# Fill order in the mixer: attention's q and k right after the k products, logits of both head parities in turn

## The chip, the cores and the metric

The kernel runs on one core of a Trainium2 chip, in one launch. The metric is the device time of that launch in microseconds. Three runs of the kernel before took 934.95, 940.38 and 941.58 us; the median is 940.38 us.

## What is computed

The reference is two transformer-like blocks on 256 tokens of width 1024, all in fp32. Only the mixer of the first block is touched by the change. Its input is normalised and multiplied by `w_in` (1024 x 3600), and the product is cut into pieces: attention's q, k, v (512 columns each), the 1536 columns that a causal convolution of width 4 and SiLU turn into q, k, v of a gated delta net, 512 columns of a gate z, and two small ones.

- Attention has 8 heads of 64. With 256 tokens there is one block of keys, so it is plain causal softmax attention with a bias by distance: `softmax(q k^T / 8 + bias) v`.
- The delta net has 8 heads of 64 and chunks of 64 tokens. Per chunk and head it forms `K K^T` under a decay, inverts a unit lower triangular 64 x 64 matrix, forms `Q K^T` under the decay, and then runs a scan over the four chunks, in which each chunk's state follows from the one before.
- Both outputs go, side by side, through `w_out`, a norm and a residual. The MLP of the first block and the whole second block follow and are the same in both kernels.

## The kernel before

**Products in three parts.** Each fp32 product with a large weight is made of three fp32r products: weight and activation are each split into a high part (a copy rounded to fp32r) and a low part (the rest). A weight slice of 128 x 1024 numbers comes by one DMA on SP's queue (`raw`, 3 buffers), ScalarE makes the high part `wh` (L146), VectorE the low part `wl` (L149); there are 6 buffers of each. `gemm_ch_steps` (L279) computes 128 output columns for all 256 tokens with one such slice: 24 matmuls (8 rows of `w_in` blocks times 3), half a PSUM bank. Two slices fill a bank, and then an evacuation runs. This document calls the work on one slice a piece. `gemm_tok_steps` works the other way around, with 12 matmuls of 512 columns to a slice.

**Two streams.** The delta net's own code stands in order in the body: decay factors, transposes and norms of k, the products `K K^T` and their mask (tile `m`), the inverse, transposes and norms of q, `Q K^T` (tile `at`), and the scan. Beside it runs a generator, `fill` (L653), which yields the wide products and attention, each with a weight in us. `go(x)` (L689) takes from the generator until weights of `x` are used up, or until a mark such as "k" or "q" has come by. So `fill` gives the order of the wide work, and the list `FILL` says how much of it is put between the steps of the delta net. In the code's order the first seven pieces (convolved k, then the first three of convolved q) stand ahead of `K K^T`; one more, the last of convolved q, stands behind it, then the first piece of convolved v, and then q is transposed (`tok_major`).

**The chain around q.** `tok_major(0, t)` transposes q to token rows (L786). `inv_norm` (L789) squares on ScalarE, sums on VectorE (`ssq`, then `ms`, L383), and takes the power -1/2 on GpSimd (tile `rnq`, through `rstd`, L381). VectorE then scales q (`fq`, `qn`, `qd`), TensorE turns the results (L802), and `pair_products` (L805) forms `Q K^T`.

**The chain of the inverse.** The masked products are stored (`md`), and read back as 16 x 16 blocks (`mb`, L899). GpSimd eliminates in 15 steps of two instructions (`tmpb`, `tb`), copies the result turned (`ub`), and SP stores `td` and `ud` (L906, L907). GpSimd then multiplies `m` with two level masks, four products (tile `b`). Two rounds on TensorE (`units`) finish the inverse. In the code, `rnq` stands ahead of the elimination, and the four mask products stand between it and `qn`.

**Attention.** `att_in(i)` makes q (i = 0, 1) or k (i = 2, 3) of four heads; ScalarE copies the bank to a tile `aqk`. `logits(a, e)` (L598) takes the two heads of parity `e` among the four of group `a`: parity 0 lies on partitions 0 to 63, parity 1 on 64 to 127. It makes four matmuls of contraction 64 into two banks of the pool "at" (2 banks), adds the bias on VectorE, and normalises. Its bias tile comes by a DMA on SP (L594). `probs_T` transposes the probabilities, `att_out` multiplies with v.

**What sets the order.** The code's order is a priority, not the order of issue. A planner sorts each engine's list in advance by its own durations: an instruction that the planner thinks ready is put ahead of an earlier one that it thinks is not. On the chip each engine then keeps its list: an instruction that has to wait holds all that stands behind it on the same engine or queue. Buffers of one tag (`t`, `g`, PSUM pools `mm` of 3 banks, `sd` of 3, `at` of 2) are shared by many tiles.

Of the kernel before, what the change touches and what calls it, by code (L numbers as in the profile page):

```python
# [18 lines left out]
S = 256  # L19
# [80 lines left out]
def body(ctx: ExitStack, tc: tile.TileContext, I: dict, cst: bass.AP, out: bass.AP, dbg=None):  # L100
    nc = tc.nc
    P = 128

    def dump(name, ap):
        if dbg is not None:
            dbg(name, ap)
# [14 lines left out]
    def T2(name, dt=F32, shape=None, tag="t"):  # L121
        return xpool.tile(shape or [P, 512], dt, tag=tag, name=nm(name), bufs=SLOTS[tag])
# [4 lines left out]
    def T1(name, tag="h"):  # L127
        return xpool.tile([P, 256], F32, tag=tag, name=nm(name), bufs=SLOTS[tag])

    def sm(name, n):  # L130
        return small.tile([P, n], F32, tag=f"{name}{n}", name=nm(name))

    def bank(tag):
        return psum.tile([P, 512], F32, tag=tag, name=nm(tag), bufs=BANKS[tag])

    def mmps():
        return bank("mm")

    def sdps():
        return bank("sd")  # L140

    def atps():
        return bank("at")

    def act(o, i, f, **kw):
        nc.scalar.activation(o, i, f, **kw)  # L146
# [4 lines left out]
    def stt(o, a, s, b, op0, op1):  # L151
        nc.vector.scalar_tensor_tensor(o, a, s, b, op0=op0, op1=op1)  # L152
# [18 lines left out]
    @contextmanager  # L171
    def after(what):

        if what in last:
            with tc.issue_after(last[what].ins):
                yield
        else:
            yield
# [28 lines left out]
    def C(name):  # L207
        o, w = COFF[name]
        return CT[o // 512][:, o % 512:o % 512 + w]
# [19 lines left out]
    def mm(o, a, b, start=True, stop=True):  # L229
        nc.tensor.matmul(o, a, b, start=start, stop=stop)  # L230
# [48 lines left out]
    def gemm_ch_steps(w, c0, X, evac):  # L279

        ps = mmps()
        for f in range(2):
            late_l = len(started) < LATE_L
            H, L = load_w(w, 0, 8, c0 + f * P, P)
            o = ps[:, f * 256:(f + 1) * 256]
            for k in range(8):
                XH, XL = X.at(k)
                mm(o, H[:, k, :], XH, k == 0, False)
                mm(o, H[:, k, :], XL, False, False)
                if not late_l:  # L290
                    mm(o, L[:, k, :], XH, False, k == 7)
            if late_l:
                for k in range(8):
                    mm(o, L[:, k, :], X.at(k)[0], False, k == 7)
            if f == 1:
                evac(ps)
            piece()
            yield 2.6
# [233 lines left out]
    QT, KT = [None] * 2, [None] * 2  # L532
# [3 lines left out]
    def qkv(i):  # L536

        def conv_evac(ps):
            acc = T2("acc", tag="j")
            y = T2("y", tag="n")  # L540
            xp = [ps[:, j * S:(j + 1) * S] for j in range(2)]
            a = [acc[:, j * S:(j + 1) * S] for j in range(2)]
            for j in range(2):
                act(a[j], xp[j], AF.Copy, scale=tap1(3, 2 * i + j))
            for tap, sh in ((2, 1), (1, 2), (0, 3)):
                for j in range(2):
                    stt(a[j][:, sh:], xp[j][:, :S - sh], tap1(tap, 2 * i + j), a[j][:, sh:], MUL, ADD)
            last["y"] = nc.scalar.activation(y, acc, AF.Silu)
            Y[i] = y.rearrange("p (j n) -> p j n", j=2)
            dump(f"y{i}", y)  # L550

        yield from gemm_ch_steps(w_in, 1536 + 256 * i, X, conv_evac)

    def att_in(i):
        def qk_evac(ps):
            s_ = T2("aqk")
            act(s_, ps, AF.Copy)
            (QT if i < 2 else KT)[i % 2] = s_.rearrange("p (a n) -> p a n", a=2)

        yield from gemm_ch_steps(w_in, 256 * i, X, qk_evac)  # L560

    def z_in():
        def z_evac(t, ps):
            Z[t] = T2("z")
            act(Z[t], ps, AF.Silu)

        yield from gemm_tok_steps(w_in, 3072, X, z_evac)

    def v_in():
        def v_evac(t, ps):  # L570
            V[t] = T2("av")
            act(V[t], ps, AF.Copy)

        yield from gemm_tok_steps(w_in, 1024, X, v_evac)
# [4 lines left out]
    def bias_in():  # L579
        relT = const.tile([32, 8], F32, name="relT")  # L580
        with after("pow"):
            nc.gpsimd.dma_start(relT, I["rel_bias"].rearrange("h b -> b h"))
        vps = sdps()
        mm(vps[:8, :256], relT, C("hot")[:32, :])
        vec = T2("vec", tag="j")
        nc.gpsimd.memset(vec, NEG)
        nc.vector.tensor_copy(vec[:8, 127:383], vps[:8, :256])
        nc.sync.dma_start(vd, vec[:8, :])

    def bias_tile(a, e):  # L590

        v = vd[:, :]
        b = T2("bias")
        nc.sync.dma_start(b, bass.AP(tensor=v.tensor, offset=v.offset + (4 * a + e) * 512,  # L594
                                       ap=[[1, P], [1024, 2], [1, 256]]))
        BIAS[a, e] = b.rearrange("p (a k) -> p a k", a=2)[:, :, ::-1]

    def logits(a, e):  # L598

        er = slice(e * 64, (e + 1) * 64)  # L600
        pl0, pl1 = atps(), atps()
        for j in range(2):
            q_, k_ = QT[a][er, j, :], KT[a][er, j, :]
            mm(pl0[:, j * P:(j + 1) * P], q_[:, 0:P], k_[:, 0:P])
            mm(pl1[:, j * S:(j + 1) * S], q_[:, P:S], k_)
        bs = BIAS[a, e]
        lg0, lg1 = T1("lg0", "k"), T2("lg1")
        l0 = lg0.rearrange("p (j k) -> p j k", j=2)
        l1 = lg1.rearrange("p (j k) -> p j k", j=2)
        stt(l0, pl0[:, 0:S].rearrange("p (j k) -> p j k", j=2), 0.125, bs[:, :, P:S], MUL, ADD)  # L610
        stt(l1, pl1.rearrange("p (j k) -> p j k", j=2), 0.125, bs, MUL, ADD)
        nm_, sm_, rs_ = sm("nmx", 4), sm("sme", 4), sm("rse", 4)
        nc.vector.tensor_reduce(nm_[:, 0:2], l0, axis=AX.X, op=MAX, negate=True)
        nc.vector.tensor_reduce(nm_[:, 2:4], l1, axis=AX.X, op=MAX, negate=True)
        for j in range(2):
            act(l0[:, j, :], l0[:, j, :], AF.Exp, bias=nm_[:, j:j + 1], accum_out=sm_[:, j:j + 1])
            act(l1[:, j, :], l1[:, j, :], AF.Exp, bias=nm_[:, 2 + j:3 + j], accum_out=sm_[:, 2 + j:3 + j])
        nc.vector.reciprocal(rs_, sm_)
        for j in range(2):
            nc.vector.tensor_scalar(l0[:, j, :], l0[:, j, :], rs_[:, j:j + 1], None, op0=MUL)  # L620
            nc.vector.tensor_scalar(l1[:, j, :], l1[:, j, :], rs_[:, 2 + j:3 + j], None, op0=MUL)
        LG[a, e] = l0, l1
        yield 1.3

    def probs_T(a, e):
        l0, l1 = LG[a, e]
        pt0, pt1 = T2("pt0"), T1("pt1", "k")
        pp, pp1 = atps(), atps()
        for j in range(2):
            nc.tensor.transpose(pp[:, j * S:j * S + P], l0[:, j, :], ident)  # L630
            nc.tensor.transpose(pp[:, j * S + P:(j + 1) * S], l1[:, j, 0:P], ident)
            nc.tensor.transpose(pp1[:, j * P:(j + 1) * P], l1[:, j, P:S], ident)
        act(pt0, pp, AF.Copy)
        act(pt1, pp1[:, 0:S], AF.Copy)
        PT[a, e] = pt0.rearrange("p (j n) -> p j n", j=2), pt1.rearrange("p (j n) -> p j n", j=2)
        yield 0.7
# [16 lines left out]
    def fill():  # L653
        yield from qkv(2)
        yield from qkv(3)
        yield "k"
        yield from qkv(0)
        bias_in()
        yield from qkv(1)
        yield "q"  # L660
        yield from qkv(4)
        yield from qkv(5)
        yield "v"
        bias_tile(0, 0)
        yield from att_in(0)
        yield from att_in(2)
        yield from logits(0, 0)
        bias_tile(0, 1)
        yield from att_in(1)
        yield from logits(0, 1)  # L670
        bias_tile(1, 0)
        yield from z_in()
        yield "z"
        yield from probs_T(0, 0)
        yield from att_in(3)
        yield from logits(1, 0)
        bias_tile(1, 1)
        yield from probs_T(0, 1)
        yield from v_in()
        yield from logits(1, 1)  # L680
        yield from att_out(0)
        yield from probs_T(1, 0)
        yield from w_out_steps(2)
        yield from probs_T(1, 1)
        yield from att_out(1)
# [300 lines left out]
    for t in range(2):  # L986
# [5 lines left out]
        for c in range(2):  # L992
            cr = slice(c * 64, (c + 1) * 64)
            pw = sdps()
            for h in range(8):
                hc = slice(h * 64, (h + 1) * 64)
                e, a = h % 2, h // 2
# [30 lines left out]
    for t in range(2):  # L1028
        po = sdps()
        vn = USB[t]  # L1030
        for c in range(2):
# [11 lines left out]
            if n < 3:  # L1043
# [4 lines left out]
                for e in range(2):  # L1048
                    er = slice(e * 64, (e + 1) * 64)
# [182 lines left out]
    for i in range(4):  # L1232
# [9 lines left out]
        for j in range(2):  # L1242
            f = 2 * i + j
            a = acc[:, j * S:(j + 1) * S]
# [141 lines left out]
```

## Time and profile before

| what | value |
|---|---|
| runs | 934.95, 940.38, 941.58 us; median 940.38 |
| the profiled execution | 941.93 us, of which the span of instructions is 940.0 |
| TensorE busy in the span | 913.8 us (97%) |
| VectorE, ScalarE, GpSimd busy | 559.6, 453.2 and 94.4 us |
| mean granted TensorE clock | 0.993 of full |
| the mixer in the trace | from about 10 us to about 198 us |

Busy shares are means over very different stretches. The mixer is a fifth of the span; the rest is long products in which TensorE never stops. In the rows below a time is microseconds from the start of the span, and "[1.81 <-DVE qn L149]" at the end of a row means that the engine stood idle for 1.81 us before it, until an instruction of VectorE that writes `qn` had ended. Matmuls overlap, so the distance from one start to the next, and not the duration, says what one costs.

### The profile page before, as it was taken

To read this page: it belongs to the slowest core of one execution; us is meant where nothing else is said; L and a number is where in the kernel's file an instruction comes from. 1 tells how busy PE (TensorE), PEld (TensorE's weight loads), DVE (VectorE), ACT (ScalarE), POOL (GpSimd) and SP (SyncE) were. 2 spreads that over 40 slices of the span, in tenths; PEclk is the share of its full clock that TensorE was granted. 3 is DMA by queue.
4 is the path that set the end of the run, shared out by engine and by line. 5 is a ranking of instruction groups with operands and counts; after the bars stand their busy time and mean duration, and the time that the engine had idled before them with its cause. 6 is when DMAs were issued, how large, how long until landed. Compare 5 with 4: busy or idle time off the path is not lost.

```text
span 940.0 us, 15151 instructions
## 1 busy us (share of the span) xinstructions
PE 913.8 (97%) x6096; PEld 812.4 (86%) x6096; DVE 559.6 (60%) x770; ACT 453.2 (48%) x639; POOL 94.4 (10%) x127
## 2 busy tenths in 40 slices
PE   7797999999999999999999999999999999999997
PEld 7697887778999888799988899988888789999886
DVE  3776535486766544768666675645457656555443
ACT  4744464256655443654545554345344545444432
POOL 4187001130000000203200000000000000000000
PEclk9999899999999999999999999999999999999999
DMA  8685542156765666577645466566474567665551
GB/s 216 183 198 148 146 157 90 45 162 174 215 189 190 215 192 197 155 217 210 181 115 176 133 176 184 163 209 191 157 235 142 172 194 201 186 187 185 182 177 45
DMA packets 176870, 161.98 MB, mean 172 GB/s; under 512 B 18916, under 2 KB 144152, under 8 KB 176800
## 3 DMA queue, kind: packets, MB, share of 16 engines
q1 hardware_dynamic: 174912, 155.96, 56.6%
q0 software_dynamic: 1728, 4.78, 1.6%
q8 instruction: 48, 0.79, 0.4%
q10 hardware_dynamic: 160, 0.27, 0.1%
q14 instruction: 22, 0.18, 0.0%
HBM read 158.07 MB, written 2.92 MB: 171 GB/s over the span
## 4 chain that ended last, share of the span: by engine, by line
PE 86%; DMA 4%; DVE 4%; ACT 2%; issue 2%; POOL 1%; SPq 0%; POOLq 0%; ACTq 0%; DVEq 0%
PE mm L230 71%; PE at L230 8%; PE sd L230 7%; DMA raw<-in_w_in_dram 3%; DVE wl L149 1%; DVE acc L152 1%; ACT wh L146 1%; PE sd L802 1%; DMA hs<-in_dec_b_dram 1%; DMA raw<-in_w_up_dram 1%; ACT junk L405 0%; PE sd L1195 0%; POOL r L410 0%; POOL rnk L149 0%; POOL rnq L149 0%
## 5 line engine op out<-in xcount | busy, mean ns | idle before, releaser
L149 DVE TENSOR_TENSOR wl<-raw,wh 128x1024 fp32r<-128x1024 f32 x285 | 348.4, 1227 | 263.5 <-ACT wh L146 262.2
L146 ACT ACTIVATE wh<-raw 128x1024 fp32r<-128x1024 f32 x287 | 302.2, 1056 | 352.3 <-PE mm L230 125.6
L230 PE MATMUL mm<-xTh,wh 128*128 128x256 f32 x960 | 273.1, 286 | 0.2
L230 PE MATMUL mm<-xTl,wh 128*128 128x256 f32 x960 | 272.4, 285 | 0.3 <-DVE xTl L475 0.2
L230 PE MATMUL mm<-xTh,wl 128*128 128x256 f32 x960 | 268.8, 285 | 0.0
L230 PEld LDWEIGHTS mm<-xTl,wh 128*128 128x128 f32 x960 | 185.3, 193 | 1.6 <-DVE xTl L475 0.7
L230 PEld LDWEIGHTS mm<-xTh,wh 128*128 128x128 f32 x960 | 185.2, 193 | 0.8 <-ACT xTh L474 0.6
L230 PEld LDWEIGHTS mm<-xTh,wl 128*128 128x128 f32 x960 | 183.4, 193 | 0.7 <-issue 0.5
L230 PE MATMUL mm<-wh,xTh 128*128 128x512 f32 x264 | 104.0, 394 | 1.2 <-ACT xTh L394 1.2
L230 PE MATMUL mm<-wh,xTl 128*128 128x512 f32 x264 | 103.2, 391 | 1.5 <-DVE xTl L397 1.5
L230 PE MATMUL mm<-wl,xTh 128*128 128x512 f32 x264 | 103.3, 391 | 0.0
L230 PE MATMUL mm<-wh,hidh 128*128 128x512 f32 x162 | 63.3, 391 | 0.1
L230 PE MATMUL mm<-wl,hidh 128*128 128x512 f32 x162 | 63.3, 391 | 0.0
L230 PE MATMUL mm<-wh,hidl 128*128 128x512 f32 x162 | 63.0, 389 | 0.0
L230 PEld LDWEIGHTS mm<-wh,xTl 128*128 128x128 f32 x264 | 49.6, 188 | 12.9 <-DVE xTl L397 2.8
L230 PEld LDWEIGHTS mm<-wh,xTh 128*128 128x128 f32 x264 | 49.6, 188 | 12.3 <-ACT xTh L394 1.9
L230 PEld LDWEIGHTS mm<-wl,xTh 128*128 128x128 f32 x264 | 49.6, 188 | 10.4 <-DVE wl L149 0.5
L410 POOL TENSOR_TENSOR r<-ms,neghalf 128x1 f32<-128x1 f32 x13 | 9.8, 757 | 462.0 <-DVE ms L152 462.0
L230 PEld LDWEIGHTS mm<-wh,hidl 128*128 128x128 f32 x162 | 30.4, 188 | 6.4
L230 PEld LDWEIGHTS mm<-wh,hidh 128*128 128x128 f32 x162 | 30.5, 188 | 6.3 <-issue 0.5
L230 PEld LDWEIGHTS mm<-wl,hidh 128*128 128x128 f32 x162 | 30.5, 188 | 5.6
L405 ACT ACTIVATE junk<-x 128x512 f32<-128x512 f32 x18 | 11.3, 626 | 18.7 <-DVE x L149 12.9
(374 smaller groups left out, 1149.8 us busy)
## 6 DMA issues: line engine op xcount, KB each, us to landing
raw<-in_w_in_dram SPq DMA_DIRECT2D x116, 512.0 KB, 4.5
raw<-in_w_up_dram SPq DMA_DIRECT2D x32, 512.0 KB, 4.5
raw<-in_w_down_dram SPq DMA_DIRECT2D x32, 512.0 KB, 4.3
raw<-in_w_ff_gate_dram SPq DMA_DIRECT2D x22, 512.0 KB, 4.0
raw<-in_w_ff_up_dram SPq DMA_DIRECT2D x22, 512.0 KB, 4.5
raw<-in_w_ff_down_dram SPq DMA_DIRECT2D x22, 512.0 KB, 3.6
raw<-in_w_r_out_dram SPq DMA_DIRECT2D x16, 512.0 KB, 3.8
raw<-in_w_out_dram SPq DMA_DIRECT2D x8, 512.0 KB, 3.5
```

The source lines that it names most:

```text
L146: nc.scalar.activation(o, i, f, **kw)
L149: (eng or nc.vector).tensor_tensor(o, a, b, op=op)
L152: nc.vector.scalar_tensor_tensor(o, a, s, b, op0=op0, op1=op1)
L230: nc.tensor.matmul(o, a, b, start=start, stop=stop)
L405: last["sq"] = nc.scalar.activation(T2("junk", tag="j"), srcs[i], AF.Square, scale=1.0 / 32, accum_out=ss[:, i:i + 1])
L410: last["pow"] = nc.gpsimd.tensor_tensor(r, ms, neghalf[:, :1], op=ALU.pow)
L802: nc.tensor.transpose(ps[:, a * P:(a + 1) * P], src[:, a * P:(a + 1) * P], ident)
```

## The change

Two things change, both in the mixer's fill.

First, `fill` yields attention's q of group 0 and k of group 0 (`att_in(0)`, `att_in(2)`) directly after the convolved k, and only then the convolved q and v. Four pieces move ahead of the four of convolved q. What stood behind moves up: the logits of group 0 come right at the mark "v", those of group 1 come together, and z and v are taken in earlier `go` calls. The loads of two bias tiles move one place up as well. `FILL` is not changed, and "att" is a mark for which no `go` asks.

Second, the matmuls of a group's logits are issued together by a new function `logits_mm`. The parities alternate from matmul to matmul, and each has its own banks: for the first 128 queries two banks of the pool "at", for the other 128 two banks of the pool "mm", which the wide products use. The softmax code on VectorE and ScalarE is as before.

```diff
+    LP = {}
+    def logits_mm(a):
+        pl0, pl1 = (atps(), atps()), (mmps(), mmps())
+        for lo in (True, False):
+            for j in range(2):
+                for e in range(2):
+                    er = slice(e * 64, (e + 1) * 64)
+                    q_, k_ = QT[a][er, j, :], KT[a][er, j, :]
+                    if lo:
+                        mm(pl0[e][:, j * P:(j + 1) * P], q_[:, 0:P], k_[:, 0:P])
+                    else:
+                        mm(pl1[e][:, j * S:(j + 1) * S], q_[:, P:S], k_)
+        for e in range(2):
+            LP[a, e] = pl0[e], pl1[e]
     def logits(a, e):
-        er = slice(e * 64, (e + 1) * 64)
-        pl0, pl1 = atps(), atps()
-        for j in range(2):
-            q_, k_ = QT[a][er, j, :], KT[a][er, j, :]
-            mm(pl0[:, j * P:(j + 1) * P], q_[:, 0:P], k_[:, 0:P])
-            mm(pl1[:, j * S:(j + 1) * S], q_[:, P:S], k_)
+        if e == 0:
+            logits_mm(a)
+        pl0, pl1 = LP[a, e]
...
         yield "k"
+        yield from att_in(0)
+        bias_in()
+        yield from att_in(2)
+        yield "att"
         yield from qkv(0)
-        bias_in()
         yield from qkv(1)
         yield "q"
         yield from qkv(4)
         yield from qkv(5)
         yield "v"
         bias_tile(0, 0)
-        yield from att_in(0)
-        yield from att_in(2)
+        bias_tile(0, 1)
         yield from logits(0, 0)
-        bias_tile(0, 1)
+        yield from logits(0, 1)
         yield from att_in(1)
-        yield from logits(0, 1)
         bias_tile(1, 0)
         yield from z_in()
         yield "z"
         yield from probs_T(0, 0)
         yield from att_in(3)
+        bias_tile(1, 1)
         yield from logits(1, 0)
-        bias_tile(1, 1)
+        yield from logits(1, 1)
         yield from probs_T(0, 1)
         yield from v_in()
-        yield from logits(1, 1)
         yield from att_out(0)
```

## Rows read from the trace of the kernel before

**Rows 1.** The page: busy time, share of the span and instructions of each engine.

```profile
PE 913.8 (97%) x6096; PEld 812.4 (86%) x6096; DVE 559.6 (60%) x770; ACT 453.2 (48%) x639; POOL 94.4 (10%) x127
```

**Rows 2.** Stretches: length, then PE, PEld, DVE, ACT, POOL busy; PEclk, DMA share, GB/s.

```profile
60.00:80.00 20.00, 17.07 (x150) 16.44 (x148) 14.88 (x30) 11.26 (x18) 14.68 (x28) 1.00 0.72 195
80.00:100.00 20.00, 17.34 (x149) 15.71 (x150) 9.73 (x14) 7.40 (x14) 8.39 (x13) 0.86 0.83 192
100.00:120.00 20.00, 20.00 (x260) 17.21 (x256) 11.61 (x22) 7.67 (x17) 1.05 (x2) 0.97 0.44 129
```

**Rows 3.** Waits of PE from 60 to 110 us: total, times, longest.

```profile
PE at L230 <- ACT aqk L146: 2.7, 1, 2.7
PE sd L802 <- DVE qn L149: 1.8, 1, 1.8
PE sd L802 <- ACT qt L146: 1.1, 1, 1.1
```

**Rows 4.** Timeline of ACT: start, duration, operation, and what ended the idle time before.

```profile
92.59 1.06 ACT L146 ACTIVATE wh<-raw 128x1024 fp32r<-128x1024 f32 x1 [0.45 <-DMA raw<-in_w_in_dram]
93.55 0.58 ACT L146 ACTIVATE aqk<-mm 128x512 f32<-128x512 f32 x1
```

**Rows 5.** The stretch after that wait, columns as in Rows 2.

```profile
94.10:99.40 5.30, 5.22 (x19) 4.28 (x19) 2.84 (x5) 2.57 (x7) 0.00 (x0) 0.53 1.04 222
```

**Rows 6.** Timeline of PE: one logits group, and two kinds of small products.

```profile
110.04 1.57 PE L230 MATMUL at<-aqk,aqk 64*128 64x128 f32 x8
80.10 1.54 PE L230 MATMUL sd<-qt,kt 64*64 64x64 f32 x32
144.17 1.14 PE L230 MATMUL sd<-us,at 64*64 64x64 f32 x16
```

**Rows 7.** Timeline of POOL around the elimination.

```profile
58.91 1.17 POOL L185 DMA_DIRECT2D wb<-in_post_mix_norm_dram  x2
...
63.08 3.29 POOL L149 TENSOR_TENSOR rnq<-ms,neghalf 128x8 f32<-128x8 f32 x2 [1.94 <-DVE ms L383]
68.03 0.23 POOL L149 TENSOR_TENSOR tmpb<-mb,tb 128x15 f32<-128x15 f32 x1 [1.65 <-DMA mb<-md]
...
69.30 1.11 POOL L149 TENSOR_TENSOR tmpb<-mb,tb 128x39 f32<-128x39 f32 x1
...
82.11 1.21 POOL L149 TENSOR_TENSOR tb<-tb,tmpb 128x15 f32<-128x15 f32 x1
...
83.96 5.05 POOL L149 TENSOR_TENSOR b<-m,cs 128x512 f32<-128x512 f32 x4
```

**Rows 8.** Timeline of DVE between the power and the scaled q.

```profile
66.70 2.43 DVE L152 SCALAR_TENSOR_TENSOR acc<-mm,chan,acc 128x255 f32<-128x255 f32 x6
69.04 1.27 DVE L149 TENSOR_TENSOR wl<-raw,wh 128x1024 fp32r<-128x1024 f32 x1
...
73.92 0.68 DVE L149 TENSOR_TENSOR qn<-sd,fq 128x512 f32<-128x512 f32 x1
```

**Rows 9.** Timeline of SP's queue: a bias load, and the store behind the elimination.

```profile
56.64 0.57 SPq L594 DMA_DIRECT2D bias<-vd  x1
...
83.34 0.37 SPq L906 DMA_DIRECT2D td<-tb  x1
```

**Rows 10.** Timeline of PE: the last transposes of convolved q to token rows.

```profile
60.58 0.61 PE L786 MATMUL sd<-ident,y 128*128 128x128 f32 x4
```

**Rows 11.** PE in the next 12 us, only matmuls into mm: length, busy, PEclk, DMA.

```profile
60.90:73.00 12.10, 11.99 (x98) 1.00 0.94 252
```

**Rows 12.** Timeline of DVE in the scan's last step and the last norm.

```profile
177.97 0.69 DVE L149 TENSOR_TENSOR us<-us,sd 64x512 f32<-64x512 f32 x1 [4.27 <-PE sd L230]
...
182.28 0.69 DVE L1016 TENSOR_REDUCE oss<-sq 128x8 f32<-128x512 f32 x1 [2.12 <-ACT sq L146]
...
185.65 0.69 DVE L149 TENSOR_TENSOR og<-og,z 128x512 f32<-128x512 f32 x1
```

**Rows 13.** The same for slices of 512 columns: length, PE, PEld, DVE, ACT; PEclk.

```profile
111.50:120.00 8.50, 8.45 (x36) 6.68 (x36) 0.00 (x0) 0.00 (x0) 1.00 0.65 194
```

## The prediction

> **What bounds the kernel now.** The page comes first: TensorE (PE) is busy 97% of the span [rows 1]. So a change can win only where PE stands still, where its clock is low, or where its work becomes less. The table by stretches finds those places. From 60 to 100 us PE is busy 17 of 20 us, from 100 to 120 all of it, and the clock is 0.86 of full from 80 to 100 [rows 2]. What ended PE's waits is the third view: from 60 to 110 us there are three long ones [rows 3]. Two belong to q's chain (1.81 us for `qn`, 1.12 us for `qt`). The longest, 2.65 us, is the first logits waiting for ScalarE's copy `aqk` of attention's k. That copy is 0.58 us of work; on ScalarE's list it stands behind the split of three weight slices [rows 4], and those slices came late because SP, whose queue is in order, stood at the store of the eliminated blocks until 83.34 us [rows 9]. After the wait PE ran 5.30 us at a mean clock of 0.53, that is mostly at 1.2 instead of 2.4 GHz [rows 5]; it cost 5.30 x (1 - 0.53) = 2.5 us. From about 100 us to the mixer's end PE hardly stops, so time won or lost before that reaches the end whole, as long as the rest stays full. All of this is in one execution of 941.93 us, 1.55 above the median of 940.38; I make the sum as a difference and add it to the median.
>
> **The copy's wait goes.** With k and q of group 0 made four pieces earlier, their copies are done long before the mark "v". The first logits then find their inputs: -2.65 us. The slow stretch behind it goes too, -2.5 us, but it comes back behind the next long wait (below).
>
> **The logits in pairs.** A group of eight instructions takes 1.57 us [rows 6], four groups 6.3 us. The trace has no contraction of 64 with 128 columns out and alternating row halves. The nearest row is `Q K^T`, which does alternate halves and banks: 32 instructions in 1.54 us, 48 ns each; the scan's product, which stays on one half, takes 1.14 us for 16, 71 ns each [rows 6]. At that ratio, 0.68, the four groups lose 6.3 x 0.32 = 2.0 us. Bounds: 0, if the pairs run one after the other, and 3.1, if they halve; I take -2.0. The Trainium skill, in "TensorEngine Tiling (Array Packing)", section Theoretical Speedup, gives up to 2x for a contraction of 64; by that rule the term would be 3.1, and the sum 1.1 lower. The rows show 1.5x for smaller products, so I stay with it. Other costs of this part: two of three banks of `mm` are held until VectorE has added the bias. The next piece takes the third bank and z comes two pieces later, so I price it at nothing; without those pieces it would be at most one piece, 2.9 us. VectorE's and ScalarE's softmax work is the same. The bias loads on SP move up one place and cost what they did, 0.6 us of issue each [rows 9].
>
> **The q chain moves behind the elimination.** This is where the change moves most. Between `K K^T` and the transposes of q the code now has six pieces and not two. A piece is 24 matmuls; 98 of them took 11.99 us [rows 11], 0.12 each, 2.9 a piece. So the transposes that ended at 60.95 us [rows 10] end 4 x 2.9 = 11.5 us later, at 72.5. The products of k, their store, and the load of the blocks do not move: the elimination still starts at 68.03, when its DMA lands [rows 7].
>
> What does GpSimd do first? Before, it had `rnq` at 63.08 and the elimination behind it [rows 7]; the loads of `wb`, which the code has only behind the whole mixer, stand ahead of both. So the planner does put later work of GpSimd ahead of work that isn't ready. Ready `rnq` is now 11.5 us later, and by the planner's durations the whole elimination ends before that: the store on SP was planned ahead of the next weight load, which waits on pieces made about 10 us after `rnq`. So I expect `rnq` behind the 30 instructions of the elimination. On the chip these end late: at 82.11 + 1.21 = 83.3. Five of them took 1.1 to 1.3 us where the others take 0.2 to 0.3 [rows 7]; the first of the five ends as VectorE's `wl` ends [rows 8]. If VectorE now stands at `fq`, waiting for `rnq`, the last three are spared, 0.9 us each: 80.7. Then come the turned copy (0.6), one mask product planned into the gap (5.05 / 4 = 1.3), and the two powers (3.3) [rows 7]: 85.9. VectorE follows with 0.3 of small scalings, six conv taps that the planner has ahead (2.43) and `qn` (0.68) [rows 8]: 89.3.
>
> And PE? From 72.5 it has pieces of convolved v, planned into the gap. There were 98 matmuls [rows 11]; now that the planner has the elimination behind it the gap is shorter. One piece, 24, is the least that the code puts there. I take 80, nearer to the row: PE stands before `qn` at 72.5 + 9.6 = 82.1. It waits 89.3 - 82.1 = 7.2 us, where it waited 1.81: +5.4. The 1.12 us for `qt` stay. The wait is followed by a slow stretch, +2.5, as after the shorter one of before [rows 5]. Bounds of the wait: 0, if `rnq` goes ahead of the elimination; and with all masks ahead (+3.8), no step spared (+2.7) and only 24 matmuls (+6.7), 20.4 us.
>
> **Other moves.** Behind `K K^T` VectorE has no conv taps in the first pieces now (2.43 us less [rows 8]) and ScalarE a copy; PE waits there for k's norm, which does not change: nothing. The weight slices are the same in number and size, one for one; nineteen of them are loaded before SP stops at the store, as far as z, so SP's stop hides behind pieces that have their weights. If SP's store were planned one slice earlier, the slice would still be needed later than 83.34 [rows 9].
>
> **Sum:** -2.65 - 2.5 + 2.5 - 2.0 + 5.4 = +0.8 us; 940.4 + 0.8 = 941.2 us.
>
> **Rival 1: the powers come first.** GpSimd's list keeps `rnq` ahead of the elimination or early in it, or PE has enough pieces planned in to cover the wait. Then -2.65 - 2.5 - 2.0 = -7.2: 933.2 us. For it: PE has attention's and z's pieces at hand. Against it: the order of `wb`.
>
> **Rival 2: the scan runs bare, slower.** Three of four v slices and a group of logits go ahead of the scan: 36 matmuls at 8.5 / 36 us = 8.5 [rows 13], and 1.6. If they are missed, each of the last two steps shows VectorE's update and the state's, some 2 us, and the last norm, its sum to its last product from 182.28 to 186.34 [rows 12] and the square ahead of them, shows 5: in all 9 us. With my wait it gives 950.2 us; without, 942. It decides once the matmuls of `w_out` that need no scan are fewer than 9 us; there are 48, by the row above 11.3 us, which speaks against it.
>
> **Rival 3: no change.** The planner sorts the lists much as before, and attention's pieces merely swap with convolved ones: 940.4 us.
>
> **Chances.** My forecast 0.50, with its own range 936 to 949 by the bounds on the wait and the logits; rival 1 0.30; rival 2 0.12; rival 3 0.08. About 1%, 9.4 us, is what a measurement of this kernel tells from no change. Slower than that needs most of the upper bound of the wait, or rival 2 on top of it: 0.11. Faster needs rival 1, halved logits and q's waits gone, 2.65 + 2.5 + 3.1 + 2.9 = 11.2: 0.09. Within 1%: 0.80. The range that holds eight in ten goes from rival 1 to rival 2, 931 to 950.
>
> **What would show it.** Right: no wait of the first logits on `aqk`; on GpSimd `rnq` behind the last `tb`; a wait of 5 to 10 us of PE for `qn`, ended by VectorE, and low clock behind it; 16 instructions of logits in 2.1 us. Wrong: `rnq` before `tmpb`; no wait above 2 us between 60 and 110; waits of PE for `us` or `og` in the scan. The prediction falls if GpSimd's list is other than I read it from the place of `wb`.

## The result: slower by 1.2%, and the profile after

The changed kernel takes 950.27 us (median of 4 runs, 947.29 to 952.75); the kernel before 939.13 (4 runs). The ratio is 1.0122, with a 95% interval of [1.0073, 1.0171]. The forecast was 941.2, in a range from 931 to 950. The profiled execution has a span of 948.8 us, 8.8 more than before, at a mean granted clock of 0.983 (before 0.993).

The page's busy line, against [rows 1]: TensorE is busy 4.5 us longer, and it has as many instructions. So it did the same work more slowly.

```profile
PE 918.3 (97%) x6096; PEld 815.6 (86%) x6096; DVE 559.2 (59%) x770; ACT 454.3 (48%) x639; POOL 93.6 (10%) x127
```

PE's waits from 20 to 215 us (total, times, longest), against [rows 3]:

```profile
PE sd L817 <- DVE qn L149: 4.5, 1, 4.5
PE sd L801 <- ACT y L548: 3.1, 1, 3.1
PE sd L230 <- ACT us L146: 2.7, 1, 2.7
PE sd L817 <- DVE kn L149: 2.5, 2, 1.9
PE sd L230 <- DVE R L149: 2.1, 1, 2.1
```

The wait for `aqk` is gone. The one for `qn` has grown from 1.8 to 4.5, and two are new: `y` (convolved q, at 74 us) and `us` (ahead of the scan, at 153). Those for `kn` and `R` stand outside the window of rows 3; the kernel before has them too, 2.5 and 2.3 us. In slices of 4 us, with the granted clock as the third number from the right, against [rows 2, 5]:

```profile
84.00:88.00 4.00, 0.00 (x0) 0.00 (x0) 2.10 (x5) 3.63 (x6) 2.04 (x2) 0.95 0.34 131
88.00:92.00 4.00, 3.86 (x12) 2.42 (x12) 3.90 (x10) 1.14 (x3) 0.00 (x0) 0.50 0.93 215
92.00:96.00 4.00, 4.00 (x48) 3.14 (x48) 0.00 (x0) 1.34 (x3) 0.00 (x0) 0.50 1.29 221
96.00:100.00 4.00, 4.00 (x34) 3.11 (x32) 1.84 (x5) 1.91 (x2) 0.00 (x0) 0.50 0.18 27
100.00:104.00 4.00, 4.00 (x17) 3.35 (x17) 3.85 (x9) 2.46 (x11) 0.00 (x0) 0.50 0.00 0
104.00:108.00 4.00, 4.00 (x34) 4.00 (x34) 1.91 (x4) 2.42 (x7) 0.00 (x0) 0.92 0.00 0
...
152.00:156.00 4.00, 3.03 (x64) 3.04 (x64) 1.23 (x1) 2.22 (x6) 0.00 (x0) 0.55 0.72 239
156.00:160.00 4.00, 4.00 (x30) 3.65 (x26) 0.84 (x2) 0.60 (x2) 0.97 (x2) 0.50 0.14 54
160.00:164.00 4.00, 4.00 (x14) 3.08 (x12) 0.00 (x0) 0.60 (x1) 0.25 (x1) 0.67 0.00 0
```

This is where most of the time went. Behind the wait for `qn` PE is busy, yet at 1.2 GHz from 88 to 104 us: first with transposes and small products, from 100.8 us on with wide ones. Behind the wait for `us` it happens again. I add up PE's busy time times (1 - clock) over the slices from 12 to 212 us that are below 0.97: 14.0 us after (8.2 behind `qn`, 4.7 behind `us`, 1.1 behind `y`), 4.5 before. The sum overstates a little, since small products do not take twice as long at half the clock: 48 of `Q K^T` took 2.59 us here, and 1.55 at full clock in the kernel with extra matmuls below. The waits that come to over 1 us from 15 to 215 us make 16.6 after and 11.9 before. Slow stretches and waits thus add 14.2 us, more than the 9.6 us by which the first transposes behind the mixer moved (197.81 to 207.39 us); the halved logits of group 1 give back 1.6 of the difference, and the rest I did not take apart.

GpSimd's timeline, against [rows 7], and VectorE's, against [rows 8]:

```profile
62.75 0.22 POOL L149 TENSOR_TENSOR tmpb<-mb,tb 128x15 f32<-128x15 f32 x1 [1.84 <-DMA mb<-md]
...
76.83 0.27 POOL L149 TENSOR_TENSOR tb<-tb,tmpb 128x15 f32<-128x15 f32 x1
77.16 0.62 POOL L920 COPY ub<-tb 128x256 f32<-128x256 f32 x1
77.75 5.05 POOL L149 TENSOR_TENSOR b<-m,cs 128x512 f32<-128x512 f32 x4
82.76 3.28 POOL L149 TENSOR_TENSOR rnq<-ms,neghalf 128x8 f32<-128x8 f32 x2
```

```profile
86.07 0.17 DVE L936 TENSOR_SCALAR fq<-rnq 128x8 f32<-128x8 f32 x1 [1.44 <-POOL rnq L149]
86.18 1.23 DVE L149 TENSOR_TENSOR wl<-raw,wh 128x1024 fp32r<-128x1024 f32 x1
...
87.40 0.68 DVE L149 TENSOR_TENSOR qn<-sd,fq 128x512 f32<-128x512 f32 x1
```

The powers `rnq` stand behind the whole elimination and all four masks. VectorE waits for them, and has a weight slice's `wl` (its low part) ahead of `qn`. That slice's load stood on SP behind the store of `td`:

```profile
77.12 0.37 SPq L921 DMA_DIRECT2D td<-tb  x1
77.81 0.66 SPq L922 DMA_DIRECT2D ud<-ub  x1
78.58 1.65 SPq L214 DMA_DIRECT2D raw<-in_w_in_dram  x2
```

The logits on PE, against [rows 6], at 83 to 90 us those of group 0 and at 136 us those of group 1:

```profile
82.95 0.71 PE L230 MATMUL at<-aqk,aqk 64*128 64x128 f32 x8
88.14 1.11 PE L817 MATMUL sd<-ident,qn 128*128 128x128 f32 x4 [4.47 <-DVE qn L149]
89.19 1.22 PE L230 MATMUL mm<-aqk,aqk 64*128 64x256 f32 x2
...
135.84 0.71 PE L230 MATMUL at<-aqk,aqk 64*128 64x128 f32 x8
136.38 1.03 PE L230 MATMUL mm<-aqk,aqk 64*128 64x256 f32 x8
```

Group 1 (the last two lines) takes 1.57 us from 135.84 to 137.41 for sixteen instructions, where two calls of the old `logits`, eight instructions each, took 2 x 1.57: exactly half. In group 0 the planner put the wide ones in twos between the transposes of q. There they ran at half the clock, two in 1.22 us where eight took 1.03, which is more than the clock alone explains: they gained nothing from being pairs.

### The profile page after: what moved, and what is told of

The parts are those of the page before. It is cut to its first block, busy times and chain, and to the rows that moved or that the text cites. A ratio compares the mean times of both kernels' runs of the same rounds, so it can differ in the third digit from the quotient of the medians.

```text
span 948.8 us, 15140 instructions
## 1 busy us (share of the span) xinstructions
PE 918.3 (97%) x6096; PEld 815.6 (86%) x6096; DVE 559.2 (59%) x770; ACT 454.3 (48%) x639; POOL 93.6 (10%) x127
## 4 chain that ended last, share of the span: by engine, by line
PE 82%; DMA 6%; DVE 4%; POOL 3%; ACT 2%; issue 2%; SPq 0%; POOLq 0%; ACTq 0%; DVEq 0%
PE mm L230 67%; PE at L230 7%; PE sd L230 6%; DMA raw<-in_w_in_dram 3%; DVE wl L149 1%; PE sd L817 1%; POOL tb L149 1%; ACT wh L146 1%; DMA bias<-vd 1%; POOL r L410 1%; DMA raw<-in_w_up_dram 1%; POOL tmpb L149 1%; POOL b L149 1%; ACT junk L405 0%; DMA mb<-md 0%
```

## The experiments

All ratios are against the kernel before, which ran beside each. The times are medians; the waits are those of one profiled execution.

| kernel | us | ratio, interval | PE's waits: qn, y, us (us) |
|---|---|---|---|
| changed | 950.27 | 1.0122 [1.0073, 1.0171] | 4.5, 3.1, 2.7 |
| order alone | 946.86 | 1.0066 [1.0042, 1.0090] | 8.9, 0.2, - |
| pairs alone | 941.55 | 1.0004 [0.9987, 1.0020] | 1.9, -, - |
| masks behind powers | 950.0 | 1.0114 [1.0078, 1.0150] | 3.4, 2.9, 2.4 |
| stores by GpSimd | 952.1 | 1.0121 [1.0097, 1.0144] | 11.5, 0.4, 3.2 |
| both of these | 953.74 | 1.0137 [1.0099, 1.0174] | 5.9, 3.5, 2.8 |
| masks early | 940.7 | 0.9998 [0.9979, 1.0016] | 1.4, 0.7, 2.8 |
| **powers first** | **931.95** | **0.9911 [0.9881, 0.9942]** | 1.4, 3.0, - |

### The two parts alone

Order alone keeps the old `logits`; pairs alone keeps the old `fill` but draws each group's two `logits` together (group 0 is shown):

```diff
-        yield from logits(0, 0)
         bias_tile(0, 1)
-        yield from att_in(1)
+        yield from logits(0, 0)
         yield from logits(0, 1)
+        yield from att_in(1)
```

> Only the first part of the change: the new fill order, logits head parity by head parity as before. Theory A: the waits at q stay and the halved logits are lost: the changed kernel's 950.3 plus 1 to 3, about 952. Rival (the pairs and their banks of the pool mm make the slowdown): near the kernel before, 938 to 942.

> Only the second part: the old fill order, with the logits of both parities together (the second parity's logits stand next to the first's, and with them two bias loads come one place earlier). Theory A: q's chain is as before, the logits halve, 16 instructions in 1.5 us and not 3.1, -3.1 in all: 936 to 938. Rival (the pairs cost by holding two banks of mm): 943 or more, with a wait of TensorE for a bank of mm.

Order alone makes about half of the slowdown. Its 946.86 is 5 us below theory A's figure, so the pairs do not gain on top of it and seem to cost, though the two intervals overlap; its wait for `qn` is 8.9 us. Pairs alone gains nothing (theory A missed, and so did its rival): the wait for `aqk` is gone, but the planner put the inverse's product in that place, and PE waits there for the eliminated blocks:

```profile
PE sd L230 <- DMA U<-ud: 4.4, 2, 4.1
```

### What holds `qn`

First the masks behind the powers; then the two stores by GpSimd; then both. In these three the lists of TensorE, VectorE and ScalarE are the changed kernel's. The lines that give the powers the name `rnq` are left out here and below.

```diff
-            with after("sub"):
+            with after("rnq"):
                 tt(h8(b), h8(MM[t]), cb(f"lev{s}"), MUL, nc.gpsimd)
...
-    nc.sync.dma_start(in_blocks(td), tb)
-    nc.sync.dma_start(in_blocks(ud), ub)
+    nc.gpsimd.dma_start(in_blocks(td), tb)
+    nc.gpsimd.dma_start(in_blocks(ud), ub)
```

> The changed kernel with one edit: the four mask products on GpSimd (5.05 us) stand behind the two powers, not ahead of them; the lists of the other engines stay as they are. Theory A (GpSimd's order made the wait for qn, and that wait the long slow-clock stretch behind it): rnq starts 5 us earlier, at about 77.8, qn at about 82.4, ahead of the point at which TensorE came to stand (83.7). The wait of 4.5 us goes to below 1, and the slow stretch from 88 to 104 us, which cost 8.2 us, shrinks. 950.3 - 4.5 - 4 = 942, and 937.5 if the whole stretch goes. Rival (the slowdown is made elsewhere, by the moved loads or the paired logits): TensorE waits as long for something else, 949 to 951.

> The changed kernel with one edit: the two stores of the eliminated blocks are issued by GpSimd, right behind the elimination, and not by SP, so SP goes on loading weight slices; the masks stay ahead of the powers, and the lists of TensorE, VectorE and ScalarE stay as they are. Theory T (two chains end together and each alone holds qn: the powers behind elimination and masks, and the weight slice's low part that VectorE has ahead of qn, behind SP's stop at the store): the slices come some 8 us earlier, but the powers end at 86 plus the two issues on GpSimd, about 87.5, and qn starts at about 89. The wait stays, 4 to 6 us; 948 to 952. Rival S (SP's stop alone holds qn): the wait falls below 1 us; 938 to 942.

> The changed kernel with both edits: the masks behind the powers, and the two stores issued by GpSimd and not by SP. Theory T: the powers end at about 82.5, the low part is done by then, qn at about 84, where TensorE comes to stand: a wait below 1 us, and the slow stretch from 88 to 104 us goes. 950.3 - 4 - 8 = 938, 935 to 941. Rival (the wait for qn is set by something that neither edit touches): the wait stays over 3 us and the time at 946 or more.

Theory A alone fell: with the masks behind, the median is 950.0 us. Four of the five runs took 946.8 to 952.3 us at clocks of 0.986 to 0.980; the profiled one took 942.4 at 0.992, so its rows show how the lists meet but not the slow stretches of the others. `rnq` did start at 77.84 and the second `fq` at 81.16, but VectorE then stood for the weight slice, and `qn` came only 0.37 us sooner than in the changed kernel:

```profile
84.35 1.59 DVE L149 TENSOR_TENSOR wl<-raw,wh 128x1024 fp32r<-128x1024 f32 x1 [1.94 <-ACT wh L146]
85.87 1.23 DVE L149 TENSOR_TENSOR fqd<-fq,ec 128x8 f32<-128x8 f32 x1
87.03 0.68 DVE L149 TENSOR_TENSOR qn<-sd,fq 128x512 f32<-128x512 f32 x1
```

The stores by GpSimd alone gave 952.1, as theory T said of the time (rival S fell); the profiled wait, 11.5 us, is longer than it said, since the stores took 1.2 us each of GpSimd and the elimination ended 3.1 us later (the blocks landed at 66.81 us in that execution, and at 62.75 in the changed kernel's). But both together gave 953.74, and theory T fell too. VectorE and GpSimd in that run:

```profile
85.36 0.98 DVE L936 TENSOR_SCALAR fq<-rnq 128x8 f32<-128x8 f32 x1 [1.98 <-POOL rnq L384]
86.97 3.66 DVE L936 TENSOR_SCALAR fq<-rnq 128x8 f32<-128x8 f32 x1 [0.64 <-POOL rnq L384]
90.55 1.21 DVE L149 TENSOR_TENSOR wl<-raw,wh 128x1024 fp32r<-128x1024 f32 x1
91.69 1.22 DVE L149 TENSOR_TENSOR fqd<-fq,ec 128x8 f32<-128x8 f32 x1
92.83 0.68 DVE L149 TENSOR_TENSOR qn<-sd,fq 128x512 f32<-128x512 f32 x1
```

```profile
83.64 3.29 POOL L384 TENSOR_TENSOR rnq<-ms,neghalf 128x8 f32<-128x8 f32 x2
86.91 5.97 POOL L149 TENSOR_TENSOR b<-m,cs 128x512 f32<-128x512 f32 x4
```

A scaling of 128 x 8 numbers that takes 0.17 us in the changed kernel takes 3.66 here. It begins 0.06 us behind the first mask product and ends as the third of the four ends (they start 1.22 us apart). The masks were not taken out of q's chain: behind the powers they hold VectorE. The `fq` of 0.98 us stands beside a power and no mask; what held it is not shown, since beside a power it took 0.17 in the changed kernel. The next kernel was to move the masks behind `qd` as well, but GpSimd's list came out the same and the masks did not wait for `qd`, so nearly the same thing ran again:

```diff
-            with after("rnq"):
+            with after("qd"):
```

> The kernel with masks behind the powers and stores by GpSimd, and one more edit: the four masks stand behind the last scaled q (qd) on VectorE as well. In the run without it VectorE's small scalings fq and fqd took 0.98, 3.66 and 1.22 us where they take 0.16 alone, all while GpSimd multiplied by masks, and qn came 6.2 us behind the end of the powers. Theory P (GpSimd's masks hold VectorE's small instructions, so moving them behind the powers only moved the delay): fq and fqd back at 0.2, qn 2 us behind the powers, TensorE's wait 5.9 to below 2 us; 953.7 - 4 - 4 (half of the slow stretch) = 945, 939 to 948. Rival (VectorE waits there for something else): the small scalings stay long, 950 or more.

949.85 us (1.0104 [1.0077, 1.0131]); `fq` and `fqd` again took 0.98, 3.67 and 1.22 us, the last two beside masks. Its theory is not tested by it.

### GpSimd's and SP's lists alone

The masks go ahead of the elimination, and its first step behind them. The planner then puts the powers into the elimination and the stores behind three more weight slices; the other three engines keep the changed kernel's lists.

```diff
+            last["mask"] = nc.gpsimd.tensor_tensor(h8(b), h8(MM[t]), cb(f"lev{s}"), op=MUL)
...
-        tt(tmp[:, :n, :w], ...)
+        with after(None if j else "mask"): tt(tmp[:, :n, :w], ...)
```

> The changed kernel with the four masks ahead of the elimination on GpSimd, where it stood idle; with them the planner puts the two powers into the middle of the elimination and SP's two stores behind three more weight slices. The lists of TensorE, VectorE and ScalarE are those of the changed kernel, instruction for instruction. Theory G (GpSimd's and SP's lists alone made the wait for qn and the slow stretch behind it): rnq at about 76, qn at about 82 with no mask beside it, TensorE's wait below 1.5 us, no slow stretch from 88 to 104: 950.3 - 4.5 - 8 = 938, 932 to 940. Rival L (the paired logits that the planner split between q's transposes are what is slow there): 946 or more.

940.7 us: theory G, 0.7 above its range; rival L fell. 9.6 us by the medians come from two lists, with not one instruction of TensorE, VectorE or ScalarE reordered; the slowest of its twelve runs (944.66) is faster than the fastest of the changed kernel's four (947.29).

```profile
59.60 6.09 POOL L915 TENSOR_TENSOR b<-m,cs 128x512 f32<-128x512 f32 x4
...
75.68 1.66 POOL L149 TENSOR_TENSOR rnq<-ms,neghalf 128x8 f32<-128x8 f32 x1 [7.53 <-DVE ms L383]
```

```profile
84.00:88.00 4.00, 4.00 (x14) 2.69 (x14) 2.34 (x6) 1.20 (x2) 3.14 (x12) 0.50 0.00 0
88.00:92.00 4.00, 4.00 (x67) 3.52 (x66) 1.57 (x4) 1.07 (x2) 1.24 (x4) 0.70 0.46 51
92.00:96.00 4.00, 4.00 (x32) 3.64 (x31) 3.86 (x9) 3.49 (x11) 0.00 (x0) 1.00 0.76 162
```

PE waits 1.4 us for `qn`, and the slow stretch costs 3.3 and not 8.2 (in the profiled run, 937.55 us). PE still waits 2.8 us for `us`, up to 143.2 us, but no slow stretch follows:

```profile
140.00:144.00 4.00, 1.22 (x47) 1.08 (x41) 1.85 (x2) 2.09 (x4) 0.00 (x0) 1.00 0.95 321
144.00:148.00 4.00, 4.00 (x73) 3.65 (x70) 0.84 (x2) 1.15 (x3) 1.02 (x2) 1.00 0.50 154
```

### Powers first: faster than both kernels

```diff
     for j in range(15):
...
-        tt(tmp[:, :n, :w], ...)
+        with after(None if j else "rnq"): tt(tmp[:, :n, :w], ...)
```

> The changed kernel with the elimination's first step behind the powers on GpSimd, the order that the kernel before had. My rival 1 put this order at 933.2 us against 940.4 before. Theory A: rnq at about 76, qn at about 81, no wait of TensorE for qn; the elimination runs about 80 to 93 and the inverse's blocks are stored at about 94, still ahead of their products (about 110). 937 to 943. Rival 1's own sum (-7.2 against before) would give 933. Rival C (the inverse becomes the late chain): a wait of 3 us or more for the blocks before the inverse's products, 944 or more.

931.95 us, below the range of theory A and within 1.3 us of my rival 1's price; rival C fell, there is no wait for the blocks. The elimination runs from 80.25 to 92.89, behind the powers:

```profile
76.99 3.29 POOL L384 TENSOR_TENSOR rnq<-ms,neghalf 128x8 f32<-128x8 f32 x2 [16.06 <-DVE ms L383]
```

Behind 80 us no slice up to 212 us is below full clock. Here the planner changed the lists of the other engines too, so the time is that of a new order on all of them.

What is left of its waits, the 3.0 us for `y` and the slow 72 to 80 us behind it, was tried next: the second bias load later, the loads of `wb` behind the masks (`"sub"` in the second pair of lines), and those behind the clearing of the state.

```diff
-        bias_tile(0, 1)
         yield from logits(0, 0)
+        bias_tile(0, 1)
...
-        with after("kd" if "kd" in last else "pow"):
+        with after("st" if "st" in last else "kd" if "kd" in last else "pow"):
```

> The kernel with the powers first (931.95 us) with the second bias tile's load back behind the first logits, so that SP does not spend 2.6 us on it ahead of three weight slices. Theory B (the wait of 3.0 us for y, and the slow clock behind it from 72 to 80 us, come from that load): both go, 3.0 + 1.7, to 927 to 929. Rival (the slices are late since the transfers themselves fill the DMA engines there): the wait for y stays over 2 us, 931 to 933.

> The kernel with the powers first (931.95 us) with one edit: the four loads of 256 KB each into wb, which GpSimd issues at 58 to 61 us and which nobody needs before 190, stand behind the masks. The second bias tile's load stays where the change put it. Theory D (the weight slices that y stands behind are late since the DMA engines are full from 60 to 72 us): the slices land some 3 us earlier, the wait of 3.0 us for y and the slow clock behind it (1.7 us) go: 926 to 929. Rival (SP's order alone made the slices late): y's wait stays near 3 us, 931 to 933.

> The kernel with the powers first, with the four loads of wb behind the clearing of the state, past the inverse; no other list changes. With them behind the masks (936.2 us) the wait for y was gone, but TensorE waited 5.6 us for the blocks U. Theory D2 (these loads, 1 MB at 100 us, held up the blocks): the wait for U falls below 2 us and y's stays gone: 927 to 931. Rival (U is late because the elimination starts only behind the powers, and TensorE now gets there 5 us earlier): the wait stays over 4 us, 934 to 937.

The bias later: 940.09 us; `y`'s wait falls only to 1.7, and PE waits 4.2 us for the logits (`lg`) that the bias now holds. `wb` behind the masks: 936.21 us; the wait for `y` is gone, so theory D is right on that wait, but one of 5.6 us for `U` takes its place. `wb` last: 932.48 us; `U`'s wait is gone too (theory D2's mechanism), yet one of 1.9 us for `aqk` appears, and the time is that of powers first. Three times the time went to what was late next.

The pairs' worth, once nothing hides it:

> The new fill order with the powers first and the logits head parity by head parity: the kernel with the powers first (931.95 us) without the pairs. Theory H (the pairs halve 6.3 us of matmuls, and TensorE is full there): 3 us slower, 934 to 936. Rival (the planner's other order in it decides): 931 to 933, or 937 and more with a wait that the other kernel does not have.

935.15 us (0.9947 [0.9929, 0.9965]) against 931.95 with the pairs: 3.2 us less with them, as theory H has it (3.1 if the logits halve), though the two intervals still overlap.

### The old order with SP freed

Stores by GpSimd in the kernel before, and that with the pairs.

> The kernel before with one edit: the two stores of the eliminated blocks are issued by GpSimd and not by SP. Theory T says that the kernel before has the same disease in another place: SP's stop made the slices and with them the copy aqk late. Its wait of 2.7 us and the slow stretch behind it go: 941 - 2.7 - 2.5 = 936, 933 to 937. Rival (another wait takes its place, as the wait for the blocks U did with the pairs alone): 939 to 942.

> The old fill order with the paired logits and the two stores issued by GpSimd. Without the pairs it took 936.56 us. Theory H: 3 us less, 933 to 934. Rival (SP or the blocks U give the gain back, as with the pairs alone): 936 to 940, with a wait for U of over 2 us.

936.56 us (0.9964 [0.9948, 0.9980]): the waits for `aqk` and the slow stretch behind it are gone, so SP's stop was that wait's cause, as the prediction read it. With the pairs 941.76 (1.0010 [0.9997, 1.0024]): the wait for `U` is 5.4 us, with the blocks stored by GpSimd, so SP's stop is not what made them late. Theory H missed: what the pairs are worth depends on what the planner moves with them.

### The wait and the clock apart

A control draws `go("v")` ahead of q's transposes; the test adds 36 matmuls whose results nobody uses ahead of the first transposes of `qn`.

```diff
+        for _ in range(n):
+            with after("vend"):
+                mm(ps[:, 0:S], X.at(0)[0][:, 0:P], X.at(0)[0])
```

> Control for the next kernel: the changed kernel with the call that takes the fill up to the mark v a few lines earlier, ahead of q's transposes; the order on the engines is nearly that of the changed kernel. 948 to 952 by every theory.

> The control with 36 matmuls whose results nobody uses (128 x 256, 0.12 us each, 4.3 us) put on TensorE right ahead of the transposes of the scaled q, where it stands still for 4.5 us. They do no work for the result. Theory K (the slow clock behind the wait costs more than the wait: about 8 us against 4.5): TensorE works through the wait, the clock stays at 1.0 behind it, and the kernel becomes faster by doing more: 941 to 945. Rival (only the wait counts; the small products behind it are slow for themselves): no gain, 949 to 953.

The control took 943.97 us (1.0043 [1.0024, 1.0061]) and not the changed kernel's 950: behind the same wait for `qn` (4.3 us) the slow stretch is there, but `us` is waited for only 0.8 us, and the slow stretch at 152 us is gone. The shorter wait is not shown to be the reason, since in masks early the stretch is gone behind a wait of 2.8. The test took 940.47 (1.0016 [0.9998, 1.0034]): 3.5 us less with 36 matmuls more. That fits theory K, but the intervals overlap, and the profiled execution, the slowest of the twelve (943.8), has the block `mb` late, so that PE waited 4.0 us all the same. The slices behind it:

```profile
92.00:96.00 4.00, 3.72 (x20) 2.81 (x20) 4.00 (x11) 1.20 (x2) 0.00 (x0) 0.57 0.48 135
96.00:100.00 4.00, 3.70 (x70) 3.04 (x68) 4.00 (x7) 3.69 (x8) 0.00 (x0) 1.00 0.45 125
```

The clock was back in one slice where the changed kernel needed four, behind a wait nearly as long; it was low again from 100 to 108 us (0.85 and 0.73). But the planner also kept group 0's sixteen logits together here, behind the transposes of q, so the test changes more than the wait.

What decides the length of a slow stretch stays open. Behind `qn` it cost 8.2 us after a wait of 4.5 (changed), 3.4 after 3.4 (masks behind powers, with the changed kernel's lists on all engines but GpSimd), and 2.2 after 8.9 (order alone). Behind `us` it cost 4.7 after a wait of 2.7, and nothing after 2.4 (masks behind powers) and 2.8 (masks early), with TensorE's list the same in all three.

## Why the prediction was wrong, step by step

- **The copy's wait, -2.65: right.** It is gone, and its cause was SP's stop.
- **The slow stretch, "-2.5, but it comes back behind the next long wait, +2.5": this step failed.** I took the size from one row of before, 5.3 us at 0.53, as if the price came with the wait. Behind the wait for `qn` it cost 8.2 us, and together the slow slices rose from 4.5 to 14.0 us. This difference of 9.5 us is by itself larger than the miss of 9.1 (950.3 against 941.2). That the split logits do not make the stretch is shown by masks early, where TensorE, VectorE and ScalarE keep their lists, the wait and its stretch are 3.1 and 4.9 us shorter, and 9.6 us come back in all. Why the stretch is so long is not shown: its length differs between kernels with the same TensorE list.
- **The q chain, +5.4: mechanism right, the size half of it.** The powers stood behind the elimination and ended at 86.04, forecast 85.9, but that was luck, by errors that cancelled: the elimination started at 62.75 and not 68.03 (the load of the blocks landed sooner; in order alone it started at 66.66), and all four masks stood ahead, not one. PE stood from 83.7 and waited 4.47, forecast 7.2, so the wait grew by 2.7; the 1.1 for `qt` did not stay. Two slips of mine changed little: 4 x 2.9 is 11.6 and not 11.5, and my own range of 936 to 949 is narrower than its bounds on the wait and the logits, which give about 933 to 956.
- **The logits, -2.0: mis-sized.** Where they stay together they halve. The Trainium skill's "TensorEngine Tiling (Array Packing)", section Theoretical Speedup, was nearer than my ratio from smaller products: 3.14 to 1.57 us in the trace. In the changed kernel the eight wide products of group 0 gained nothing.
- **Other moves, 0: wrong.** The waits for `y` (3.1) and `us` (2.7) are new. The weight slices ahead of `y` on ScalarE's list were late: in the kernel with the powers first, that wait goes once 1 MB of `wb` loads is not beside them. I priced the bias loads by their issue of 0.6 us; here the second took 2.69 (and 2.40 without the `wb` loads, so these are not its reason):

```profile
58.40 2.69 SPq L594 DMA_DIRECT2D bias<-vd  x1
61.15 5.45 SPq L214 DMA_DIRECT2D raw<-in_w_in_dram  x3
```

The copy `us` stands on ScalarE's list behind slices of `w_out`:

```profile
148.08 1.06 ACT L146 ACTIVATE wh<-raw 128x1024 fp32r<-128x1024 f32 x1 [1.45 <-DMA raw<-in_w_out_dram]
151.37 1.06 ACT L146 ACTIVATE wh<-raw 128x1024 fp32r<-128x1024 f32 x1 [2.23 <-DMA raw<-in_w_out_dram]
152.34 0.58 ACT L146 ACTIVATE us<-sd 128x512 f32<-128x512 f32 x1
```

- **The rivals.** Rival 1's price, 933.2, is near what the kernel with the powers first gave (931.95), in part by luck, since that kernel has a wait of 3.0 us for `y` that the price does not hold; its order simply was not the planner's. Rival 2's 950.2 is the measured time by luck, not by its mechanism: the list of PE's waits has none in the scan's steps, only the one for `us` ahead of them. My sign of being wrong, a wait for `us`, did come. Rival 3 is out by the ratio.

## What to carry to other kernels

Price a wait of TensorE with the stretch behind it, and as a range: here 4.5 us of waiting were followed by 16 us at half clock, while other waits of 2 to 3 us were followed by none. Before moving a chain, list everything that its last instruction has ahead of it on its own engine; here the powers, a weight slice's low part behind SP's store, and the masks on GpSimd each held `qn` in turn, and moving the masks behind the powers, freeing SP, or both, gained nothing. The lists of two engines that are nearly idle, GpSimd and SP, were worth 1% of a kernel that TensorE bounds.

## What the runs showed of the hardware

- **GpSimd's products hold VectorE's small instructions.** `fq` (128 x 8) took 0.17 us with GpSimd idle, and 1.26, 3.66 and 3.67 beside the masks, in three kernels; `fqd` 0.16, and 1.22 to 1.23. No run makes GpSimd idle there with all else the same, so it is the rows' timing that tells it. The Trainium skill, "SBUF — State Buffer", section Who interferes with whom, says that the two engines share a port pair, and that it is an exclusive lock. The rows agree, and add that the wait can last over three products in a row.
- **The scatter goes with the clock.** Twelve runs of masks early lie between 935.46 us at a mean granted clock of 0.994 and 944.66 at 0.984; a line through them falls 9.0 us for 0.01 of clock.
